# One more weight tile in the ring: nine tiles of 8 KB a partition instead of eight, in a one-core RG-LRU / gated-MLP / mixture-of-experts kernel

## The chip, the cores and the metric

The kernel runs as one program on one core of a Trainium2 chip. The metric is the device time of one execution in microseconds (us); lower is better. Engines are called by the profile's names: PE is TensorE's matmuls and PEld its weight loads, DVE is VectorE, ACT is ScalarE, POOL is GpSimd and SP is SyncE, which here issues nearly all transfers from HBM. A transfer issued by SP carries one weight tile of 1 MB (128 partitions x 2048 floats).

## The reference, cut to what matters

Two layers over 256 latent tokens of width 1024. Layer 0 mixes tokens with a bidirectional recurrent block (RG-LRU), layer 1 with a gated MLP over chunks of 128 tokens; each is followed by a mixture of experts, which is where most of the weights are.

```python
def moe_ffn(xn, router_w, router_b, w_gu, w_down, ws_gu, ws_down):   # xn: 256 x 1024
    scores = jax.nn.sigmoid(xn @ router_w)                           # 64 experts
    ...                                                              # the best 4 of 8 groups, of those the best 8 experts
    y = lax.map(expert_block, ...)       # swiglu(x_pad[tok], w_gu[e], w_down[e]) * gate
    return routed + swiglu(xn, ws_gu, ws_down)                       # and one shared expert
```

An expert has `w_gu` (1024 x 512) and `w_down` (256 x 1024) in float32: three tiles of 1 MB. All 64 experts of both layers are read once, so a mixture of experts reads 192 MB of expert tiles and 3 MB of the shared expert's.

## The kernel before, in words

**The ring.** Every weight goes through one stream, `Stream`. The order of its loads is fixed when the program is written: `moe_loads` and the lists around it call `st.add`. A load takes the slot that was freed longest ago; SP is in order, so a load whose slot is still in use holds every later load. The slots are the `RING` tiles named `wr`, and from the end of layer 0's mixer on four more named `wx`: 12 slots in both mixtures of experts, and 13 after the change. Expert loads cannot be issued before the router has written `order` (the experts in order of load), because their addresses come from it.

**A mixture of experts, `moe(l, tail)`.** Work of three kinds shares PE:

- Experts with few tokens are packed: a group `g` has four blocks of 32 token slots, from one to four experts, which run side by side on PE. `gate_up` does a group in two halves (four of eight 128-row pieces each, one `w_gu` tile per expert and half), `flip` and `down` do the second product, `gather` and `scatter` move the tokens of a batch of two groups in and out by matmuls with one-hot matrices. There are 22 groups in 11 batches, and before a batch the tiles of its experts are taken from the stream in a fixed order.
- Two experts (`NAT`) and the shared one are computed for all tokens, and so are the five experts with most tokens (`TOP`). This work is cut into pieces that can be put anywhere, the queue `ups`: per expert one entry that starts splitting its first weight tile, 16 steps of gate and up product (`over_all`, 6 matmuls a step), again an entry that starts the split, and two steps of the down product (`all_down`, 24 matmuls each).
- These dense experts use weights split in a high and a low part: `splitter` copies a quarter tile to `wh` on ACT (line 563), and POOL or DVE subtract it to give `wl` (line 564). Splitting runs two to three quarter tiles ahead of PE, but the first quarter of an expert's gate and up tiles, and of its down tile, is asked for by the entry that starts it. Below, such a first quarter is called a **restart**.

**What sets the order around the change.** While the program is written, a planner keeps a clock (`st.now`, advanced by the table `COST`) and an expected arrival for each load: 2.6 us after the later of the load before it and the moment its slot was freed. Before a piece of group work, `until` takes steps from `ups` until the tiles of that piece should have arrived:

```python
        def until(tiles):
            while ups:
                t = max(st.arrival(n) for n in tiles)
                if t <= st.now:
                    break
                ...
                up(1)
            st.now = max(st.now, max(st.arrival(n) for n in tiles))
```

So the number of slots changes not only when a load may be issued but where the dense experts' steps stand in every engine's program. Once written, the order is fixed; each engine waits by semaphores.

Of the kernel before, what the change touches and what calls it, by code (L numbers as in the profile page):

```python
# [20 lines left out]
T = 256  # L21
E = 64
EPS = 1e-6
RING = 8

NEXT = (0, 2, 2)

# [274 lines left out]
def _body(nc, tc, a, pp, rp, ps, ps1, dr):  # L302
# [334 lines left out]
    def mixer0(rx):  # L637
      with tc.tile_pool(name="m0", bufs=1) as mp, tc.tile_pool(name="m0t", bufs=2) as tp:
# [24 lines left out]
        nc.sync.dma_start(mixg, a["mix_g"])  # L663
        st.grow(rp, "wr", RING)
        for t_, n_ in ((cw, "a_cw"), (cb, "a_cb"), (rb_, "a_rb"), (ib_, "a_ib"), (lam, "a_lam")):
# [956 lines left out]
```

## Time and profile before

| | |
|---|---|
| time, median of 3 runs | 1508.54 us (1504.59 to 1512.67) |
| the profiled execution, its own time | 1504.02 us |
| span of its profile, first to last instruction | 1502.2 us |
| mean granted TensorE clock | 0.973 of 2.4 GHz |
| PE busy | 1410.3 us (94%) |
| bytes over the transfers' queues | 514.88 MB, mean 343 GB/s |
| layer 0: mixer, then mixture of experts | to about 293 us, to about 803 us |
| layer 1: mixer, then mixture of experts | to about 991 us, to about 1496 us |

The profile shows one execution. A row of a timeline gives start, duration, engine, line, operation, tiles and count; a bracket at its end says how long the engine had been idle and which instruction ended that. The clock column (PEclk) is the share of 2.4 GHz that TensorE was granted: 1.00, or 0.5 (1.2 GHz), or a mean of both over a stretch.

### The profile page before, as it was taken

To read this page: it belongs to the slowest core of one execution; us is meant where nothing else is said; L and a number is where in the kernel's file an instruction comes from. 1 tells how busy PE (TensorE), PEld (TensorE's weight loads), DVE (VectorE), ACT (ScalarE), POOL (GpSimd) and SP (SyncE) were. 2 spreads that over 40 slices of the span, in tenths; PEclk is the share of its full clock that TensorE was granted. 3 is DMA by queue.
4 is the path that set the end of the run, shared out by engine and by line. 5 is a ranking of instruction groups with operands and counts; after the bars stand their busy time and mean duration, and the time that the engine had idled before them with its cause. 6 is when DMAs were issued, how large, how long until landed. Compare 5 with 4: busy or idle time off the path is not lost.

```text
span 1502.2 us, 27457 instructions
## 1 busy us (share of the span) xinstructions
PE 1410.3 (94%) x10752; PEld 983.3 (65%) x10752; DVE 766.5 (51%) x1388; ACT 518.9 (35%) x901; POOL 433.7 (29%) x454
## 2 busy tenths in 40 slices
PE   5999898789999999999999999789999999999998
PEld 4767677546567565565747899666656666566665
DVE  6899997623343434334346686532425333333434
ACT  4767673321222222222225544422212212212232
POOL 1666665412222113221101361322212212211210
PEclk9999999899999999999999999899999999999998
DMA  9776575589998999999999854469998999999994
GB/s 376 280 278 228 224 308 224 231 318 377 381 418 358 421 420 406 421 394 420 420 418 380 320 169 153 140 231 391 362 396 358 421 421 409 406 402 422 420 420 168
DMA packets 77446, 514.88 MB, mean 343 GB/s; under 512 B 9856, under 2 KB 10240, under 8 KB 17024
## 3 DMA queue, kind: packets, MB, share of 16 engines
q1 hardware_dynamic: 74720, 508.91, 83.8%
q10 hardware_dynamic: 2592, 4.16, 0.8%
q8 instruction: 86, 1.41, 0.4%
q14 instruction: 48, 0.39, 0.1%
HBM read 511.99 MB, written 1.05 MB: 342 GB/s over the span
## 4 chain that ended last, share of the span: by engine, by line
PE 59%; issue 13%; POOL 3%; DVE 2%; DMA 2%; ACT 1%; ACTq 0%; POOLq 0%; SPq 0%; DVEq 0%
PE b L307 49%; PE s L307 10%; DMA wr<-in_m_gu 2%; POOL S L1399 1%; POOL wl L564 1%; PE b L1475 1%; DMA wr<-in_m_dn 1%; DVE wl L564 1%; DVE h L948 0%; ACT wh L563 0%; PE b L1587 0%; DVE v L1004 0%; DVE xT L1115 0%; DVE v L1067 0%; DVE u L956 0%
## 5 line engine op out<-in xcount | busy, mean ns | idle before, releaser
L564 POOL TENSOR_TENSOR wl<-wr,wh 128x512 fp32r<-128x512 f32 x134 | 208.2, 1570 | 537.0 <-ACT wh L563 534.8
L307 PE MATMUL b<-wr,xg 128*32 128x512 f32 (+2 forms) x1496 | 301.1, 602 | 8.2 <-DMA wr<-in_m_gu 6.3
L563 ACT CAST wh<-wr 128x512 fp32r<-128x512 f32 x256 | 152.4, 618 | 200.8 <-PE b L307 93.6
L307 PE MATMUL b<-wx,xg 128*32 128x512 f32 (+1 forms) x712 | 196.1, 599 | 0.0
L307 PEld LDWEIGHTS b<-wr,xg 128*32 128x32 f32 (+2 forms) x1496 | 83.3, 119 | 130.6 <-issue 107.2
L307 PE MATMUL s<-hh,wh 128*128 128x256 f32 x512 | 153.7, 300 | 6.4 <-ACT wh L563 6.4
L564 POOL TENSOR_TENSOR wl<-wx,wh 128x512 fp32r<-128x512 f32 x48 | 71.4, 1505 | 302.5 <-ACT wh L563 263.5
L1115 DVE SCALAR_TENSOR_TENSOR xT<-b,mod,xT 128x256 f32<-128x256 f32 x304 | 130.0, 478 | 49.1 <-PE b L307 43.2
L564 DVE TENSOR_TENSOR wl<-wr,wh 128x512 fp32r<-128x512 f32 x122 | 100.2, 838 | 104.3 <-ACT wh L563 104.2
L1491 DVE SCALAR_TENSOR_TENSOR Y<-b,gt,Y 128x512 fp32r<-128x512 f32 x88 | 66.1, 751 | 169.4 <-ACT Y L1490 169.4
L307 PE MATMUL s<-hh,wl 128*128 128x256 f32 x512 | 146.9, 287 | 3.4 <-POOL wl L564 3.4
L307 PE MATMUL b<-wr,ht 128*32 128x512 f32 (+2 forms) x752 | 148.1, 599 | 1.5 <-ACT ht L1477 1.4
L307 PE MATMUL s<-hl,wh 128*128 128x256 f32 x512 | 145.9, 285 | 0.0
L1468 DVE TENSOR_TENSOR h<-h,b 128x256 f32<-128x256 f32 x44 | 18.5, 420 | 205.3 <-ACT h L1467 205.3
L307 PEld LDWEIGHTS s<-hh,wh 128*128 128x128 f32 x512 | 99.4, 194 | 36.0 <-issue 28.3
L1490 ACT ACTIVATE Y<-b,gt 128x512 fp32r<-128x512 f32 x88 | 60.5, 687 | 136.0 <-PE b L307 136.0
L1467 ACT ACTIVATE h<-b 128x256 f32<-128x256 f32 x44 | 16.9, 383 | 256.4 <-PE b L307 256.4
L307 PEld LDWEIGHTS s<-hh,wl 128*128 128x128 f32 x512 | 99.4, 194 | 4.5 <-POOL wl L564 4.2
L307 PEld LDWEIGHTS s<-hl,wh 128*128 128x128 f32 x512 | 99.6, 194 | 0.4
L307 PE MATMUL b<-wx,ht 128*32 128x512 f32 (+2 forms) x352 | 99.1, 603 | 0.5 <-ACT ht L1477 0.5
L563 ACT CAST wh<-wx 128x512 fp32r<-128x512 f32 x112 | 66.5, 618 | 93.9 <-PE b L307 48.3
L1399 POOL TENSOR_SCALAR S<-cst,agq 128x32 fp32r<-128x32 f32 (+3 forms) x208 | 82.6, 421 | 49.4 <-PE b L307 49.3
(283 smaller groups left out, 2817.5 us busy)
## 6 DMA issues: line engine op xcount, KB each, us to landing
wr<-in_m_gu SPq DMA_DIRECT2D x173, 1024.0 KB, 11.6
wx<-in_m_gu SPq DMA_DIRECT2D x83, 1024.0 KB, 11.9
wr<-in_m_dn SPq DMA_DIRECT2D x82, 1024.0 KB, 10.8
wx<-in_m_dn SPq DMA_DIRECT2D x40, 1024.0 KB, 9.9
wr<-in_ada_w SPq DMA_DIRECT2D x31, 1024.0 KB, 7.8
wr<-in_a_in SPq DMA_DIRECT2D x10, 1024.0 KB, 8.7
wr<-in_ada SPq DMA_DIRECT2D x8, 1024.0 KB, 12.2
wr<-in_b_v SPq DMA_DIRECT2D x7, 1024.0 KB, 16.3
```

What stands on the lines that cost most here:

```text
L307: PE.matmul(out, lhsT, rhs, start=start, stop=stop, skip_group_check=True)
L563: S.copy(out=hi, in_=t)
L564: eng(i, c).tensor_tensor(out=lo, in0=t, in1=hi.bitcast(F32), op=OP.subtract)
L1115: V.scalar_tensor_tensor(out=xT[:, d, :], in0=y, scalar=mod[:, l, 5, d:d + 1], in1=xT[:, d, :], op0=OP.mult, op1=OP.add)
L1399: (G if b else V).tensor_scalar(out=s[:, tt, i * P + o:i * P + o + wd], in0=C["iota1"][:, j:j + wd], scalar1=agq[:, tt, q:q + 1], scalar2= ...
L1467: S.activation(out=h, in_=p[:, :256], func=AF.Silu)
L1468: V.tensor_tensor(out=h, in0=h, in1=p[:, 256:], op=OP.mult)
L1475: PE.transpose(p[:, k * P:(k + 1) * P], h[:, k * P:(k + 1) * P], ident)
L1490: S.activation(out=hi, in_=p, func=AF.Copy, scale=gts[g])
L1491: V.scalar_tensor_tensor(out=y[:, 1, 512 * c:512 * c + 512], in0=p, scalar=gts[g], in1=hi.bitcast(F32), op0=OP.mult, op1=OP.subtract)
```

## The change

`RING` becomes 9, and the program is built with 1 KB a partition set aside for the descriptors of transfers that GpSimd issues, instead of the builder's default, which makes room for the 8 KB of the ninth tile. The kernel issues no transfer from GpSimd. No arithmetic changes, and no transfer is added or removed.

```diff
-RING = 8
+RING = 9
...
-    nc = bacc.Bacc("TRN2", target_bir_lowering=False, num_devices=1)
+    nc = bacc.Bacc("TRN2", target_bir_lowering=False, num_devices=1, dynamic_dma_scratch_size=1024)
```

The planner then writes a different order. Three places are shown, all in layer 0's mixture of experts; layer 1's has the same differences.

SP, the start of the expert loads. `wr` and `wx` are ring tiles, `order` is the router's list and `flag` the word that tells whether an expert has more tokens than its slots. Before, the last load ahead of the wait for `flag` (the fourth):

```order
L382 DMA wx_2611<-in_m_gu 128x2048
L374 TENSOR_LOAD order
L374 ISA x2
L382 ISA
L382 DMA wr_2681<-in_m_gu 128x2048
L1357 TENSOR_LOAD flag
```

With nine:

```order
L382 DMA wr_2611<-in_m_gu 128x2048
L374 TENSOR_LOAD order
L374 ISA x2
L382 ISA
L382 DMA wr_2622<-in_m_gu 128x2048
L374 TENSOR_LOAD order
L374 ISA x2
L382 ISA
L382 DMA wx_2692<-in_m_gu 128x2048
L1357 TENSOR_LOAD flag
```

A fifth expert tile is loaded ahead of the flag; every later load has moved one place up against the work that frees slots.

ACT, around the first four-expert group. `hf` and `fh` end the gate and up product of a dense expert, `wh` is the high part of a split quarter tile, `h` and `ht` belong to a group's activation and transpose, `xg` is a gather's result, `Y` a down product's. Before:

```order
L1170 ACTIVATE hf<-s 128x512
L1174 CAST fh<-hf 128x512
L563 CAST wh<-wx_2217 128x512 x4
L1467 ACTIVATE h<-b 128x256
L1477 COPY ht<-b 128x256
L1415 COPY xg<-b 128x512
L1490 ACTIVATE Y<-b,gt 128x512 x2
L1477 COPY ht<-b 128x256
L1415 COPY xg<-b 128x512
L563 CAST wh<-wx_2284 128x512
```

With nine:

```order
L1170 ACTIVATE hf<-s 128x512
L1174 CAST fh<-hf 128x512
L1467 ACTIVATE h<-b 128x256
L1477 COPY ht<-b 128x256
L1415 COPY xg<-b 128x512
L1490 ACTIVATE Y<-b,gt 128x512 x2
L1477 COPY ht<-b 128x256
L1415 COPY xg<-b 128x512
L563 CAST wh<-wr_2139 128x512 x3
L1490 ACTIVATE Y<-b,gt 128x512 x2
```

The restart of the next dense expert (`wx_2217`, and `wr_2139` with nine) has moved from right behind the end of the one before it to behind the second gather.

PE, the third of the five top experts. `s<-hh` and `s<-hl` are its last gate and up step, `b<-fh` and `b<-fl` the first matmuls of its down product, and `b<-wx,xg` a group's gate and up matmuls. Before:

```order
L307 MATMUL s<-hh,wh 128x256
L307 MATMUL s<-hl,wh 128x256
L307 MATMUL s<-hh,wl 128x256
L307 MATMUL b<-fh,wh 128x256
L307 MATMUL b<-fl,wh 128x256
L307 MATMUL b<-fh,wl 128x256
```

With nine:

```order
L307 MATMUL s<-hh,wh 128x256
L307 MATMUL s<-hl,wh 128x256
L307 MATMUL s<-hh,wl 128x256
L307 MATMUL b<-wx_6075,xg 32x512
L307 MATMUL b<-wr_6154,xg 32x512
L307 MATMUL b<-wr_6165,xg 32x512
```

A half group (16 such matmuls) now stands between the end of this expert's first product and the start of its second.

## Rows read from the trace of the kernel before

**Rows 1.** The page: busy time, and the granted clock in 40 slices of the span.

```profile
PE 1410.3 (94%) x10752; PEld 983.3 (65%) x10752; DVE 766.5 (51%) x1388; ACT 518.9 (35%) x901; POOL 433.7 (29%) x454
PEclk9999999899999999999999999899999999999998
```

**Rows 2.** Stretches of layer 0's experts: length, busy time (and count) of five engines, clock, DMA share, GB/s.

```profile
314.50:781.90 467.40, 454.71 (x3632) 292.60 (x3634) 178.91 (x333) 114.93 (x207) 97.12 (x138) 0.99 0.98 403
470.00:535.00 65.00, 64.97 (x479) 39.49 (x471) 23.43 (x44) 15.31 (x28) 12.11 (x23) 1.00 1.01 421
535.00:782.00 247.00, 241.00 (x1973) 156.59 (x1975) 96.31 (x181) 61.07 (x110) 49.34 (x66) 0.99 1.00 414
```

**Rows 3.** Timeline of SP, which only issues: start, duration of the issue, tiles.

```profile
276.28 0.34 SPq L382 DMA_DIRECT2D wx<-in_m_gu  x1
297.19 0.34 SPq L382 DMA_DIRECT2D wr<-in_m_gu  x1
300.63 0.34 SPq L382 DMA_DIRECT2D wr<-in_m_gu  x1
309.72 0.33 SPq L382 DMA_DIRECT2D wx<-in_m_gu  x1
310.31 1.52 SPq L382 DMA_DIRECT2D wr<-in_m_gu  x3
```

**Rows 4.** The chain that ended last: start, duration, and what it was then.

```profile
300.63 4.62 DMA wr<-in_m_gu
311.48 12.00 DMA wr<-in_m_gu
327.46 10.25 DMA wr<-in_m_dn
729.25 7.21 PE s L307 x60
1091.53 3.57 PE b L307 x32
```

**Rows 5.** Timeline of PE, layer 0, first four-expert group.

```profile
305.29 1.06 PE L307 MATMUL b<-wr,xg 128*32 128x512 f32 x1 [2.34 <-DMA wr<-in_m_gu]
316.96 0.38 PE L307 MATMUL s<-hh,wh 128*128 128x256 f32 x1 [2.02 <-ACT wh L563]
318.32 0.38 PE L307 MATMUL s<-hh,wl 128*128 128x256 f32 x1 [0.86 <-POOL wl L564]
```

**Rows 6.** Waits of PE, layer 1, 995 to 1042 us: total, times, longest.

```profile
PE b L307 <- DMA wr<-in_m_gu: 2.4, 1, 2.4
```

**Rows 7.** Timeline of PE, layer 0, later restarts.

```profile
384.65 0.39 PE L307 MATMUL s<-hh,wh 128*128 128x256 f32 x1 [1.19 <-ACT wh L563]
386.00 0.39 PE L307 MATMUL s<-hh,wl 128*128 128x256 f32 x1 [0.85 <-POOL wl L564]
568.03 0.38 PE L307 MATMUL b<-fh,wh 128*128 128x256 f32 x1 [1.19 <-ACT wh L563]
635.82 0.39 PE L307 MATMUL b<-fh,wh 128*128 128x256 f32 x1 [2.74 <-ACT wh L563]
637.18 0.58 PE L307 MATMUL b<-fh,wl 128*128 128x256 f32 x1 [0.75 <-POOL wl L564]
```

**Rows 8.** Stretches around those rows, columns as in rows 2.

```profile
301.20:311.00 9.80, 7.46 (x36) 1.81 (x33) 1.33 (x4) 0.32 (x1) 0.00 (x0) 0.83 0.37 115
383.00:391.00 8.00, 5.96 (x38) 3.72 (x41) 2.42 (x3) 2.76 (x5) 6.33 (x11) 0.79 0.95 377
566.00:574.00 8.00, 5.96 (x47) 5.55 (x47) 4.43 (x8) 2.76 (x5) 5.95 (x9) 1.00 1.02 424
632.00:644.00 12.00, 8.51 (x50) 6.58 (x52) 5.86 (x9) 4.01 (x7) 4.20 (x3) 0.72 1.01 413
```

**Rows 9.** Waits of PE, layer 0, 535 to 790 us: total, times, longest.

```profile
PE b L307 <- ACT wh L563: 3.9, 2, 2.7
PE b L307 <- POOL wl L564: 1.6, 2, 0.9
```

## The prediction, made before the changed kernel had run

> **What bounds the kernel now.** I read the page first: PE is busy 94% of the span, and its granted clock is nearly always full [rows 1]. PE is therefore the engine to watch, and a change to loads can only pay where PE waits for a load. The kernel's mixers are left out for that reason; the ring is stretched to its limit in the two mixtures of experts, where the queue runs at 0.98 of its time at 403 GB/s (the first row of [rows 2]).
>
> Next, stretches of layer 0's experts. From 470 to 535 us both sides are full: PE 64.97 of 65 us, the queue 421 GB/s. From 535 to 782 the queue still moves 414 GB/s and PE is busy 241 of 247 us [rows 2]. Two things full at once do not tell which one waits for the other, so the waits decide. In 535 to 790 us PE waited for splits of dense experts (ACT `wh`, POOL `wl`: 3.9 and 1.6 us) and never for a load worth a row [rows 9]. At the start of the experts it did wait for loads: 2.34 us before 305.29 in layer 0 [rows 5], 2.4 us in layer 1 [rows 6], and the chain runs over transfers there three times [rows 4]. So loads bound the first 40 us or so of each mixture, PE's own order of work the rest.
>
> One full-rate tile takes 1.0486 MB / 421 GB/s = 2.49 us. A lone tile lands 4.62 us after its issue [rows 4]. A half of a four-expert group costs PE 3.57 us, and one dense step 7.21 / 10 = 0.72 us [rows 4].
>
> **The change, part by part.** *(a) The fifth expert tile ahead of the flag.* Before, SP issues three expert tiles up to 276.28, a fourth soon after, and the next at 297.19, when the first group has freed a slot; the one that PE then waits for goes at 300.63 [rows 3]. With nine, the tile of 297.19 is already in, and the awaited one takes its place: 297.19 + 4.62 = 301.8, before 302.95 (305.29 - 2.34), where PE ran dry. The gap of 2.34 us goes [rows 5], and with it the half-rate clock behind it: 9.8 us at 0.83 cost 1.7 us [rows 8]. The half that ended in the release of 309.72 [rows 3] now ends 4.0 us earlier, at 305.7.
>
> That release sends the second half's tiles. Before, four were issued, the last landing at 311.48 + 12.00 = 323.48 [rows 4]; now one of them went early, and the third of a release lands 323.48 - 2.49 - 309.72 = 11.3 us behind it, at 317.0. The half starts 6.5 us earlier. But the planner has taken three dense steps (2.2 us) out of the fill in front of it, because it books 2.6 us a tile and not the 4.62 of a queue that had run dry. Six steps (4.3 us) end near 310, so **PE idles some 6 us for loads where it idled 2.02 + 0.86 us for a restart** [rows 5]. After that the half clock (1.2 GHz) is likely: 0 to 1.7 us.
>
> The down tiles follow the next release as before (327.46 + 10.25, [rows 4]) and keep the lead; the restart that moved behind the second gather is covered by that wait. One more step is put off. Gain of layer 0: 6.5 less four deferred steps (2.9) less 0 to 1.7 = 1.9 to 3.6, I take 2.7. Layer 1 has the gap [rows 6] but I found no slow clock behind it: 2.4 + 2.5 - 2.9 less 0 to 1.7 = 0.3 to 2.0, taken as 1.1. Together **3.8 us (2.2 to 5.6)**.
>
> *(b) The restarts.* PE's work does not change, so from there on only its idle time and clock count. In layer 0 before, after the first group: one restart behind a gather at 384 (1.19 + 0.85 us, and 8 us at 0.79 of the clock, 1.7 us), one behind a gather at 568 (1.19 and a POOL part of 1.6 - 0.75 = 0.85 us, clock full), and the third top expert's, directly behind the end of its own first product (2.74 + 0.75, and 12 us at 0.72, 3.4 us) [rows 7 to 9]. Sum 3.7 + 2.0 + 6.9 = 12.6 us. None of these three stands there with nine: the first follows a down product, the second a half group comes between, the third likewise.
>
> The new order exposes five. Two down products begin right behind the end of another expert's first product, as the restart of [rows 5] did: 2.88 us each. Two top experts begin behind a gather: 2.04 us each. The one behind a down product is not in the trace: at least 1 us (a copy on ACT has to wait for that product's `Y`), at most 2.04; I take 1.5, since ACT has less queued than behind a gather. Sum 11.3 us. The clock: after the four long gaps of layer 0 before it fell to a cost of 1.7, 0 and 3.4 [rows 8] and some in the first; I take 1.7 in two of the five (14.7 us), none to all five (11.3 to 19.8). Against 12.6 that is 2.1 us lost a layer (1.3 won to 7.2 lost), **4.2 us lost in both (2.6 won to 14.4 lost)**.
>
> *(c) The rest, at nothing.* The small transfers that now stand behind a ninth tile at the program's start land one tile later, 2.49 us if nothing covered it; I take nothing, since their first use comes later than that. The smaller area for GpSimd's descriptors costs nothing, since the kernel gives GpSimd no transfer. Earlier loads of the late experts are worth nothing while PE does not wait for them; if PE got far ahead, the full queue would be next (403 of 421 GB/s).
>
> **Sum:** 3.8 - 4.2 = 0.4 us slower, between 8.2 us faster and 12.2 us slower. The sum is made on the profiled execution, 1504.02 us; the median of the runs shown is 1508.54, 0.3% above it, and I put the same difference on it: **1509 us**. This measurement cannot tell less than 0.5% (7.5 us) from no change.
>
> **The rivals.** *Restarts fall well:* the clock stays full and the exposed restarts coincide with waits for loads. Both upper bounds then hold, 8.2 us, 1500 us. For it: the clock did stay full at 568 [rows 8]. Against it: PE is late there, not the loads. Chance 0.2.
>
> *The queue's idle time comes back:* between 314.5 and 781.9 us the queue moves 403 and not 421 GB/s, so it loses 467.4 x (1 - 403/421) = 20 us a layer; if loads bound the layer, a deeper ring gives both back: 1509 - 40 = 1469 us. Against it stands the list of waits without a load [rows 9]. The Trainium skill (Perfetto Trace Analysis, Optimization Strategy) says that consistent bubbles on the engine that should be saturated can mean that there is not enough SBUF for the next tile. By that rule the change should win; here the bubbles of PE after 535 us end with a split, not with a load, so the trace agrees only for the start. Chance 0.1.
>
> *Slower:* the new wait of (a) recurs. The planner moves steps away from in front of tiles wherever it now expects them sooner, and a tile is sooner only if its slot was the limit and the queue not full. Where it was full, four deferred steps (2.9 us) turn into a wait, with 1.7 us of clock. With two such places more in each layer: 2 x 2 x 4.6 = 18 us, 1527 us. It decides from two places a layer upward. For it: 470 to 535 us, where queue and PE are both full [rows 2]. Against it: the tiles in front of which steps were taken away were bought one release earlier. Chance 0.16.
>
> *The change doesn't act:* the orders shown differ in every engine, so 0.02, same time.
>
> **How the numbers follow.** The likeliest case, no measurable change at 1509, has 0.52. Its own range is 1500 to 1521, the two ends of the sum. Faster by over 0.5% (under 1501) are the queue's case and most of the well-falling restarts: 0.1 + 0.18 = 0.28. Slower (over 1516) is 0.16; the likeliest case's tail to 1521 is small beside it. Within 0.5%: 0.56. The range 1494 to 1523 leaves out the queue's case and about half of the slow one, less than 0.2.
>
> **What would show each step.** For (a): the fifth expert tile issued before 285 us; PE's gap at 305 gone; a new gap of 5 to 7 us before the second half of the first four-expert group, ended by a load. For (b): the gap of 2.74 us at 636 gone, and gaps of 2 to 3 us at restarts elsewhere, five a layer, with the half clock behind some. I would be wrong if PE waits for loads in the middle of the experts, if the restarts are hidden or cost more than a split and a subtraction, or if PE's busy time itself falls or grows by more than the clock explains.

## The result: slower by 0.6%, and the profile after

The changed kernel takes 1516.52 us (median of 8 runs, 1515.49 to 1518.06) against 1507.26 us before (8 runs); the ratio is 1.0062, with a 95% interval of 1.0046 to 1.0078. The forecast was 1509 us in a range of 1494 to 1523. The range holds the result. The likeliest case, no change beyond 0.5%, does not: the loss is some 9 us where the sum said 0.4. It is clear of the noise: with eight runs of each kernel the interval is 0.16% to either side, finer than the 0.5% that the prediction allowed for.

The page of the changed kernel, to set beside [rows 1]; its span is 1514.8 us, against 1502.2:

```profile
PE 1410.4 (93%) x10752; PEld 979.3 (65%) x10752; DVE 769.0 (51%) x1388; ACT 518.3 (34%) x901; POOL 434.2 (29%) x454
PEclk9999999899999999999999999899999999999998
```

PE's busy time and its count are those of before, so the 12.6 us of span look like idle time. Over layer 0's experts as a whole the queue moves less than before (395 against 403 GB/s); only from 535 us on it moves a little more (418 against 414). Stretches, for [rows 2]:

```profile
314.50:787.00 472.50, 454.02 (x3609) 290.02 (x3608) 176.90 (x328) 113.70 (x205) 96.90 (x138) 0.98 0.96 395
...
535.00:787.00 252.00, 247.37 (x1996) 159.35 (x1995) 97.91 (x183) 61.14 (x111) 49.34 (x66) 0.99 1.01 418
```

**The start.** SP in the timeline, for [rows 3]; the last number is the count of issues in the row:

```profile
274.97 3.29 SPq L382 DMA_DIRECT2D wr<-in_m_gu  x4
281.96 0.34 SPq L382 DMA_DIRECT2D wx<-in_m_gu  x1
```

The fifth expert tile goes at 281.96 instead of 297.19. PE's waits in the timeline, for [rows 5] (layer 0, first two rows) and [rows 6] (layer 1):

```profile
313.98 1.04 PE L307 MATMUL b<-wr,xg 128*32 128x512 f32 x2 [2.48 <-DMA wr<-in_m_gu]
316.47 1.06 PE L307 MATMUL b<-wx,xg 128*32 128x512 f32 x1 [1.45 <-DMA wx<-in_m_gu]
...
1017.51 1.05 PE L307 MATMUL b<-wr,xg 128*32 128x512 f32 x2 [1.77 <-DMA wr<-in_m_gu]
1019.99 1.06 PE L307 MATMUL b<-wx,xg 128*32 128x512 f32 x1 [1.44 <-DMA wx<-in_m_gu]
```

The gap at 305 us is gone. The next half group waits for its tiles instead, as step (a) said. The wait is longer than its gaps: the half's own stretch, from its first matmul to its last, shows 10.60 us with 6.68 us busy; the same 32 matmuls (the program's 16, each of which the trace lists as two) take 4.60 us where nothing is waited for, at much the same clock (the first experiment below). That is 6.0 us of waiting, of which the trace books 3.9 as idle:

```profile
310.50:321.10 10.60, 6.68 (x48) 1.67 (x48) 1.38 (x2) 0.62 (x1) 0.00 (x0) 0.84 0.84 352
```

**The restarts.** PE in the timeline, for [rows 7], layer 0: the restart behind the second gather, then the five behind it.

```profile
330.65 0.39 PE L307 MATMUL s<-hh,wh 128*128 128x256 f32 x1 [1.19 <-ACT wh L563]
332.01 0.38 PE L307 MATMUL s<-hh,wl 128*128 128x256 f32 x1 [0.85 <-POOL wl L564]
...
368.92 0.39 PE L307 MATMUL b<-fh,wh 128*128 128x256 f32 x1 [2.74 <-ACT wh L563]
370.26 0.51 PE L307 MATMUL b<-fh,wl 128*128 128x256 f32 x1 [0.84 <-POOL wl L564]
394.42 0.38 PE L307 MATMUL s<-hh,wh 128*128 128x256 f32 x1 [1.37 <-ACT wh L563]
453.05 0.58 PE L307 MATMUL b<-fh,wh 128*128 128x256 f32 x1 [2.74 <-ACT wh L563]
613.45 0.39 PE L307 MATMUL s<-hh,wh 128*128 128x256 f32 x1 [1.19 <-ACT wh L563]
666.75 0.39 PE L307 MATMUL s<-hh,wh 128*128 128x256 f32 x1 [1.19 <-ACT wh L563]
```

All five stand where the order put them; layer 1 has the same five. Stretches of 10 us around them, for [rows 8]: three with the clock below 1.00 in layer 0, four in layer 1.

```profile
366.00:376.00 10.00, 6.42 (x42) 5.00 (x44) 5.75 (x9) 2.90 (x6) 2.95 (x2) 0.83 0.68 269
450.00:460.00 10.00, 6.70 (x34) 6.20 (x33) 5.99 (x11) 3.42 (x6) 2.97 (x3) 0.66 0.75 296
612.00:622.00 10.00, 7.96 (x51) 3.44 (x50) 2.59 (x4) 3.84 (x7) 6.76 (x12) 0.83 1.01 417
665.00:675.00 10.00, 7.96 (x69) 6.52 (x71) 3.24 (x4) 4.01 (x7) 6.41 (x8) 1.00 1.01 419
...
1366.00:1376.00 10.00, 7.96 (x53) 7.55 (x51) 2.67 (x4) 4.00 (x7) 5.20 (x5) 0.83 1.01 420
```

The list of PE's waits from 340 to 790 us, for [rows 9] (total, times, longest):

```profile
PE b L307 <- ACT wh L563: 5.5, 2, 2.7
PE s L307 <- ACT wh L563: 3.8, 3, 1.4
PE s L307 <- POOL wl L564: 2.5, 3, 0.9
PE b L307 <- POOL wl L564: 1.4, 2, 0.8
PE b L307 <- DVE wl L564: 0.8, 1, 0.8
...
PE b L307 <- DMA wr<-in_m_gu: 0.4, 1, 0.4
```

These are 14.0 us for splits and 0.4 for loads. One of them, 0.8 us for DVE, is no new one: the kernel before has it too. In layer 1 (1040 to 1493 us) the splits sum to 14.3 us.

### The profile page after: what moved, and what is told of

The parts are those of the page before. It is cut to its first block, busy times and chain, and to the rows that moved or that the text cites. A ratio compares the mean times of both kernels' runs of the same rounds, so it can differ in the third digit from the quotient of the medians.

```text
span 1514.8 us, 27436 instructions
## 1 busy us (share of the span) xinstructions
PE 1410.4 (93%) x10752; PEld 979.3 (65%) x10752; DVE 769.0 (51%) x1388; ACT 518.3 (34%) x901; POOL 434.2 (29%) x454
## 4 chain that ended last, share of the span: by engine, by line
PE 56%; issue 18%; POOL 3%; DVE 2%; DMA 1%; ACT 1%; ACTq 0%; POOLq 0%; DVEq 0%
PE b L307 44%; PE s L307 11%; POOL wl L564 1%; POOL S L1399 1%; DMA wr<-in_m_gu 1%; PE b L1475 1%; DVE wl L564 1%; DVE h L948 0%; DVE xT L1115 0%; DVE v L1004 0%; PE b L1587 0%; DVE v L1067 0%; DVE u L956 0%; ACT wh L563 0%; ACT h L1066 0%
## 5 line engine op out<-in xcount | busy, mean ns | idle before, releaser
L564 POOL TENSOR_TENSOR wl<-wr,wh 128x512 fp32r<-128x512 f32 x136 | 215.3, 1601 | 611.2 <-ACT wh L563 580.7
L307 PE MATMUL b<-wr,xg 128*32 128x512 f32 (+2 forms) x1440 | 307.0, 605 | 5.9 <-DMA wr<-in_m_gu 4.7
L307 PE MATMUL b<-wx,xg 128*32 128x512 f32 (+2 forms) x768 | 220.6, 603 | 3.6 <-DMA wx<-in_m_gu 2.9
L563 ACT CAST wh<-wr 128x512 fp32r<-128x512 f32 x272 | 161.5, 618 | 180.7 <-PE b L307 109.9
L564 DVE TENSOR_TENSOR wl<-wr,wh 128x512 fp32r<-128x512 f32 x136 | 117.0, 877 | 101.7 <-ACT wh L563 101.6
L564 POOL TENSOR_TENSOR wl<-wx,wh 128x512 fp32r<-128x512 f32 x46 | 65.1, 1430 | 262.0 <-ACT wh L563 222.5
L307 PE MATMUL b<-wx,ht 128*32 128x512 f32 (+2 forms) x392 | 117.8, 600 | 0.5 <-ACT ht L1477 0.5
L307 PEld LDWEIGHTS b<-wx,xg 128*32 128x32 f32 (+2 forms) x768 | 55.4, 117 | 70.8 <-issue 59.0
L307 PE MATMUL b<-S,xt 128*128 128x256 f32 x704 | 94.0, 287 | 0.0
## 6 DMA issues: line engine op xcount, KB each, us to landing
wr<-in_m_gu SPq DMA_DIRECT2D x170, 1024.0 KB, 11.8
wx<-in_m_gu SPq DMA_DIRECT2D x86, 1024.0 KB, 11.3
wr<-in_ada SPq DMA_DIRECT2D x8, 1024.0 KB, 14.4
```

Source lines behind the costliest of these rows:

```text
L307: PE.matmul(out, lhsT, rhs, start=start, stop=stop, skip_group_check=True)
L563: S.copy(out=hi, in_=t)
L564: eng(i, c).tensor_tensor(out=lo, in0=t, in1=hi.bitcast(F32), op=OP.subtract)
```

## The experiments

The change does two things, a ninth slot and a new order of steps. The theory to test (A): the slot gains at the start, and the order loses at the restarts. Its rivals: the slot or the smaller descriptor area hurts by itself (B), or loads bound the experts, so that a gain at one place is lost at the next load (C).

### The slot, the order and the descriptor area apart

Nine tiles with the order of eight: the number of entries of `ups` (dense steps, and the entries that start a split) that `until` takes at each of its 66 calls in a layer is written out as a table, taken from the kernel before.

```diff
+        steps = iter([
+            0, 0, 0, 10, 0, 2, 2, 2, 7, 3, 0, 4, 2, 2, 0, 5, 0, 2, 2, 2, 4, 7,
...
+        ])
         def until(tiles):
-            while ups:
...
+            up(next(steps))
             st.now = max(st.now, max(st.arrival(n) for n in tiles))
```

> Nine tiles in the ring, but the dense experts' steps stand where they stood with eight (the number of steps before each piece of group work is written out as a table). Theory A (the loss comes from where the reorder leaves the restarts): the splits cost what they cost before (11 to 12 us of idle PE a layer, clock at half some 8 us a layer), and the load gaps at the start of each mixture of experts (2.34 us and 2.42 plus 1.04 us) go or shrink below 1 us: 1500 to 1505 us, 3 to 7 us faster than with eight. Rival B (the ninth tile itself hurts, by its place in memory or by the transfers it adds in flight): near the changed kernel, 1514 to 1518 us. Rival C (the start gives nothing either): 1507 us as before.

Measured: 1490.36 us, ratio 0.988 (0.986 to 0.9899). The direction is A's, and B is out. The gain, 16.6 us, is far above the 3 to 7 expected, and 1490 lies outside A's range. The two halves of the second group, by stretches of this kernel:

```profile
301.10:305.80 4.70, 4.70 (x34) 1.17 (x34) 1.48 (x4) 0.56 (x2) 0.00 (x0) 1.00 0.71 253
317.20:321.80 4.60, 4.60 (x49) 1.38 (x51) 0.05 (x1) 0.00 (x0) 0.00 (x0) 0.80 0.97 367
```

Before, the first of these took some 9.5 us ([rows 8], first row), 4.8 more. The expectation counted the idle gap of 2.34 us of it; the half clock behind the gap makes some 1.7, and the last 0.8 is a wait inside PE's busy time. Over the whole execution such hidden waits are the larger part: the span is 13.2 us shorter (1489.0 against 1502.2), and of these PE's busy time gives 8.7 (1401.6 against 1410.3, [rows 1]), with the same 10752 matmuls and nearly the same mean clock (0.974 and 0.973).

Eight tiles with the order of nine (the same edit in the kernel before, with the other table):

> Eight tiles in the ring, with the dense experts' steps where they stand with nine: the reorder alone. Theory A: the same split gaps as in the changed kernel (about 16 us a layer against 11), and since a load that the new order counts on is one release later, longer load gaps at the start of each mixture of experts, 6 to 10 us a layer against 3.5: 1520 to 1536 us, slower than the changed kernel. Rival B (the ninth tile hurts by itself, the order does not): 1507 us, as before. If the reorder costs its splits and no more load time: 1516 us.

Measured: 1541.24 us, ratio 1.0226 (1.0208 to 1.0245). The waits of PE in layer 0, 300 to 804 us:

```profile
PE b L307 <- DMA wr<-in_m_gu: 7.2, 6, 2.5
PE b L307 <- ACT wh L563: 5.5, 2, 2.7
PE s L307 <- ACT wh L563: 4.9, 4, 1.4
PE s L307 <- POOL wl L564: 3.4, 4, 0.9
...
```

The split waits are those of the changed kernel (this list begins at 300 us and so has the first restart too), and load waits come on top, as A expects; the sum is 5 us above its range, again with a busy time that has grown (1429.3 us). The four corners:

| | order of eight | order of nine |
|---|---|---|
| eight tiles | 1507 us | 1541.2 us |
| nine tiles | 1490.4 us | 1516.5 us |

The ninth tile gains 17 us in one order and 25 in the other. The new order loses 34 and 26.

The descriptor area alone, cut to 1 KB with eight tiles:

> The kernel before with eight tiles and only the descriptor area cut to 1 KB. Theory A: no change, ratio 0.998 to 1.002, 1507 us, and the same gaps of PE in both mixtures of experts. Rival B (the smaller area or the moved addresses of the tiles cost time): 1510 us or more, with longer transfers or longer copies on ACT, DVE and POOL.

Measured: 1506.17 us, ratio 0.9991 (0.998 to 1.0003). No cost is to be seen.

### Where in the order the 26 us lie

Nine tiles, with the new order only at the start of each mixture of experts: the table of eight with 6 instead of 10 entries before the second group's second half, and 11 instead of 7 before the fourth group's first. (The 10 are nine dense steps and the entry that starts the next expert's split.)

```diff
-            0, 0, 0, 10, 0, 2, 2, 2, 7, 3, 0, 4, 2, 2, 0, 5, 0, 2, 2, 2, 4, 7,
+            0, 0, 0, 6, 0, 2, 2, 2, 11, 3, 0, 4, 2, 2, 0, 5, 0, 2, 2, 2, 4, 7,
```

> Nine tiles, splits as before, the new order only up to the fourth group of each mixture of experts and the order of eight from there on: the four steps that the new order takes away from in front of the second group's second half are done before the fourth group's first half. Theory A (the reorder loses little at the start and most at the five restarts after it): from 1490.4 us, load gaps of 3.9 and 3.2 us come back, the first restart costs 0.8 us less in each layer, half clock 0 to 3.4 us: 1495 to 1500 us, leaving 16 to 21 us of the reorder's 26 for the restarts after it. Rival C (the start carries most of it): 1505 us or more.

Measured: 1502.15 us, ratio 0.9968 (0.9956 to 0.9981). Of the 26.2 us the start carries 11.8 and the order behind it 14.4. That is in neither expected range, about midway between them: A is right that the order behind the start carries the larger part, and wrong that the start loses little. The list of PE's waits from 340 to 790 us for splits, to be read against the one of the changed kernel above:

```profile
PE b L307 <- ACT wh L563: 3.9, 2, 2.7
PE b L307 <- POOL wl L564: 2.2, 3, 0.8
PE s L307 <- ACT wh L563: 1.2, 1, 1.2
...
PE s L307 <- POOL wl L564: 0.8, 1, 0.8
PE b L307 <- DVE wl L564: 0.8, 1, 0.8
```

8.9 us here, 14.0 in the changed kernel: 5.1 us of idle time more; in layer 1 the same sums are 8.9 and 14.3.

The half clock differs too. In this run it stands behind two restarts in each layer, 1.7 us each time; the two of layer 0:

```profile
564.00:574.00 10.00, 7.96 (x52) 7.50 (x50) 4.66 (x9) 2.76 (x5) 7.62 (x14) 0.83 1.01 421
634.00:644.00 10.00, 8.41 (x56) 5.49 (x56) 4.38 (x7) 3.06 (x6) 4.24 (x3) 0.83 1.00 411
```

The first of these is the restart that in the trace of before kept the full clock ([rows 8], third row), in the same order of work and with the same waits. The reverse is seen in the run with the smaller area alone, where the restart at 384 us waits as before (1.19 and 0.84 us) and keeps the full clock, against 0.79 in [rows 8]:

```profile
383.00:391.00 8.00, 6.00 (x50) 3.17 (x50) 2.75 (x3) 3.45 (x6) 6.82 (x12) 1.00 0.95 373
```

So which restart is followed by the half clock is no property of the order; it changes from one execution to another.

### The restarts made earlier

The changed kernel with PE's order kept to the row. Only the first two splits of a restart move: ahead of the last two steps of the first product in front of it, or right behind the second step of the down product in front of it.

```diff
+        def early(i):
+            fn, n, cost, at = ups[i]
+            if n is not None and cost == 0.0 and st.arrival(n) <= st.now:
+                ups[i] = (lambda: None, n, 0.0, None)
+                fn()
+
         def up(n):
             for _ in range(n):
                 if ups:
+                    if len(ups) > 2 and ups[0][2] and ups[0][3] is None and ups[1][3] is None:
+                        early(2)
                     fn, tile_, cost, at = ups.popleft()
...
                     fn()
                     st.now += cost
+                    if at and ups:
+                        early(0)
```

> The changed kernel with PE's order kept, but each dense expert's first two quarter tiles are split earlier: before the last two steps of the first product ahead of it, or right behind the second step of the down product ahead of it, if the tile is expected to be there. Theory A (late splits are what the change lost): the gaps of 1.19 and 0.85 us behind gathers and of 1.37 and 0.85 us behind a down product go, those of 2.74 us shrink to 2.3 to 2.5 us, since the chain that ends the first product is nearly as long, and lose the 0.85 us behind them; 8 to 10 us of idle PE a layer and 3 to 7 us of half clock a layer: 1484 to 1498 us, below the kernel with eight. Rival C (loads bound the experts, so that what is won at a split is lost at the next load): new load gaps in the middle of the experts, 1507 us or more.

Measured: 1469.77 us, ratio 0.9747 (0.973 to 0.9764): 46.7 us below the changed kernel and 14 below A's range. PE's waits in layer 0, 300 to 767 us:

```profile
PE b L307 <- DMA wr<-in_m_gu: 2.5, 1, 2.5
PE b L307 <- DMA wx<-in_m_gu: 1.4, 1, 1.4
PE b L307 <- POOL wl L564: 0.8, 1, 0.8
PE b L307 <- DVE wl L564: 0.8, 1, 0.8
...
```

The stretch behind the start of layer 0's experts, in the changed kernel (340 to 790 us) and in this one (336.2 to 766.6, the same 3491 matmuls):

```profile
340.00:790.00 450.00, 435.02 (x3491) 279.61 (x3493) 171.62 (x321) 106.58 (x192) 90.12 (x126) 0.98 0.98 401
```

```profile
336.20:766.60 430.40, 428.26 (x3491) 279.01 (x3494) 167.06 (x321) 108.00 (x192) 88.72 (x126) 1.00 1.00 413
```

Idle time falls from 15.0 to 2.1 us, and the clock is full throughout, which takes 6.8 us off the busy time, just what the three half-clock stretches above had cost (1.7 + 3.4 + 1.7). The 2.74 us gaps go whole, against the expectation that 2.3 to 2.5 us of each would stay. ACT in the changed kernel shows why; the restart of 368.92:

```profile
365.51 0.60 ACT L1170 ACTIVATE hf<-s 128x512 f32<-128x512 f32 x1 [8.64 <-PE s L307]
367.73 0.62 ACT L1174 CAST fh<-hf 128x512 fp32r<-128x512 f32 x1 [1.62 <-DVE hf L1173]
368.25 1.66 ACT L563 CAST wh<-wr 128x512 fp32r<-128x512 f32 x3
```

The split was not waiting for its tile. It stood on ACT behind `fh`, which ends another expert's product and waits 1.62 us for DVE; the down product that restarts is that of the expert before, whose `fh` is long there. Where a down product follows its own expert's first product, the gap does stay: in nine tiles with the order of eight (below) one row has 2.22 us behind `fh` itself.

The same edit in the kernel before:

> The kernel before, eight tiles and its own order on PE, with the earlier splits of the dense experts. Theory A (restarts cost their idle time and the half clock behind it, wherever they stand): idle PE for splits falls from 11 us a layer to 2 or 3, and of the half clock behind the six long restarts (13.6 us in both layers) most goes: 1475 to 1483 us. With the run of nine tiles and earlier splits (1469.8) that leaves nine tiles with the new order 5 to 13 us ahead of eight, where it was 9 us behind. Rival C (with eight tiles the time won at splits is lost again at loads): 1490 us or more, with new load gaps.

Measured: 1492.25 us, ratio 0.9906 (0.9886 to 0.9927). A's range is missed, C's bound of 1490 is met. The waits in layer 0, 300 to 775 us:

```profile
PE b L307 <- DMA wr<-in_m_gu: 5.3, 4, 2.3
...
PE b L307 <- DMA wr<-in_m_dn: 1.4, 1, 1.4
...
```

With eight tiles PE, no longer held up at splits, runs into loads: 6.7 us against 3.1 before in this layer (300 to 783 us). So C holds for eight tiles, in part.

Nine tiles, the order of eight, and the earlier splits:

> Nine tiles, the order of eight, and the earlier splits. Theory A: from 1490.4 us, 20 us of idle PE for splits and 7 to 10 us of half clock go: 1458 to 1466 us. Against nine tiles with their own order and earlier splits (1469.8) it is faster by the load gaps at the start of each mixture of experts alone, 3.9 and 3.2 us, and up to 3.4 us of half clock. Rival B (the new order is better once its splits are hidden): 1470 us or more.

Measured: 1464.55 us, ratio 0.9727 (0.9706 to 0.9748), as A expected. The order that cost 26.2 us costs 5.2 once the splits are early. The row with `fh`:

```profile
616.81 0.38 PE L307 MATMUL b<-fh,wh 128*128 128x256 f32 x1 [2.22 <-ACT fh L1182]
```

### The planner's booking of an empty queue

The changed kernel's planner takes steps away in front of the second half of the second group because it books 2.6 us for a tile whose slot comes free when nothing is in flight. A lone tile takes 4.62 us [rows 4]. One line books 2.2 us more in that case; `open` is the time at which `order` is ready.

```diff
-            self.dma = max(self.dma, self.since.get(w, 0.0)) + LOAD
+            self.dma = max(self.dma, max(self.since.get(w, 0.0), self.open) + 2.2) + LOAD
```

With this alone:

> The changed kernel with one thing added: the planner books 2.2 us more for a load whose slot comes free when the queue has run dry; splits stay as they were. It writes ten dense steps in front of the second group's second half as the order of eight does. Theory A (the reorder was the loss, and this booking undoes it): near the run of nine tiles with the order of eight (1490.4), 1484 to 1497 us. Rival (any order planned for nine tiles leaves its restarts as badly): 1505 us or more.

Measured: 1485.81 us, ratio 0.9855 (0.9829 to 0.988), 31 us below the changed kernel and in A's range. Ten entries (nine steps) stand in front of the second group's second half again, in both layers. The line changes the order behind the start as well, so the 31 us are those of the whole order, not of this one place. With the earlier splits as well:

> Nine tiles, earlier splits, and a planner that books 2.2 us more for a load whose slot comes free when the queue has run dry (a lone tile lands 4.6 to 4.9 us after its issue in the traces). It writes ten dense steps instead of six in front of the second group's second half, and a similar order to that of eight tiles from there on. Theory A: the load gaps at the start go, the splits stay hidden: 1458 to 1466 us. Rival (they come back in front of another tile): 1469 us or more, as with nine tiles, their own order and earlier splits.

Measured: 1460.23 us, ratio 0.9692 (0.9672 to 0.9712), in A's range. PE's waits in layer 0, 300 to 761 us, and the whole of that stretch:

```profile
PE b L307 <- DMA wx<-in_m_gu: 1.4, 1, 1.4
PE s L307 <- DVE wl L564: 0.9, 1, 0.9
...
300.00:761.00 461.00, 456.40 (x3718) 291.37 (x3720) 176.56 (x337) 117.23 (x209) 93.84 (x138) 1.00 1.00 412
```

Both mends with eight tiles, and with ten. With 1 KB a partition for descriptors ten tiles do not fit, by 0.97 KB a partition; with the area cut to 32 bytes they do.

> Eight tiles with both mends, the earlier splits and the booking of an empty queue. Theory A (with splits hidden, loads at the start of each mixture of experts are what is left, and the ninth tile is worth what it was with the order held, 17 to 28 us): 1477 to 1488 us against 1460.2 with nine. Rival (the mends alone do it, the ninth tile is worth nothing once order and splits are right): 1458 to 1465 us.

> Ten tiles with both mends, the area for descriptors cut to 32 bytes a partition to make room. With nine (1460.2), PE waits for loads only 1.44 us in each mixture of experts, so a tenth can give 3 us and what clock follows: 1452 to 1460 us. Rival (the reorder by a tenth tile exposes something again): 1465 us or more.

Measured: 1475.29 us, ratio 0.9793 (0.9772 to 0.9815), with eight, a little below A's range; and 1453.64 us, ratio 0.9655 (0.9638 to 0.9672), with ten, in the expected range. With order and splits mended each further tile pays: 15.1 us for the ninth, some 6 for the tenth, each with the order that the planner writes for it. Ten tiles with both mends is the fastest version, 51 us below the kernel before on the same chip.

## Why the prediction was right in its steps and low in its sum

**What bounds the kernel: right.** Loads bound the start of each mixture, PE's own order the rest. The changed kernel waits 14.0 us for splits after 340 us and 0.4 for loads (layer 0).

**(a) The start: right in its steps; in size only as a sum, and by luck.** The fifth tile, the gap that goes and the wait of "some 6 us" that comes are all in the trace (6.0 us). Term (a) was a gain of 3.8 us, 2.2 to 5.6. The run with the new order at the start and the old one behind it measures 4.7 us (1506.83 - 1502.15). One sentence in it was wrong: the restart behind the second gather is not covered by the wait for down tiles; PE waits 1.19 and 0.85 us for its splits and for no load. The gross gain of the slot, 16.6 us, was larger than the 11.4 us that the working had (6.5 in layer 0, 2.4 + 2.5 in layer 1), and so was the cost of the steps put off, 11.8 us against 5.8 and 0 to 3.4 of clock. The two errors cancel. By layers they do not: from the first group to the place where the steps put off are made up, the same matmuls take 63.2 us before and 62.7 with the new start in layer 0, and 61.9 and 59.9 in layer 1. That is 0.4 and 2.0 us won where the term had 2.7 and 1.1.

**(b) The restarts: right in place, too small in size. This is the term that was mis-sized.** The term was a loss of 4.2 us in both layers; 1516.52 - 1502.15 = 14.4 us was measured, the far end of its range. It has two parts.

- Idle time: five restarts at 11.3 us in place of three at 7.6 us make 3.7 us a layer, 7.5 in both. The waits of the two runs differ by 5.1 and 5.4, together 10.5. The two down products behind another first product wait 2.74 us for the first split and 0.56 to 0.85 for the second, not 2.88 in sum, and the restart behind a down product 1.37 + 0.85, not 1.5 and more than the 2.04 that was named as its most.
- Clock: the term took the half clock behind two restarts a layer, 3.4 us, where before it was 5.1: a gain of 3.4 us in both. The stretches show 1.7 + 3.4 + 1.7 = 6.8 us in layer 0 (10 us at 0.83, 0.66 and 0.83) and four of 1.7 in layer 1: 13.6. The trace of before has 10.2 and that of the run with the new start 6.8, so the loss is 3.4 to 6.8 us, by the execution that it is set against.

So some 3 us of the miss are idle time and 6.8 to 10.2 are clock; with the 4.2 of the term that is 14.0 to 17.4, where the medians differ by 14.4 and the two profiled executions by 15.6 (1516.53 - 1500.97). That the late splits cause both is shown by the run with PE's order unchanged and the splits earlier: both go together there, 15.0 to 2.1 us idle and a clock of 0.98 to 1.00. How many restarts are followed by the half clock could not have been read off one trace: it changes between executions of the same order, as the rows above show.

**(c): right.** The smaller area shows no cost, 0.9991. PE reaches the first group of layer 0 at 293.82 us instead of 293.46, so in these two executions the small transfers at the program's start cost 0.4 us at most.

**The rivals.** *Restarts fall well* is out: none of the five coincided with a load. The time lies just inside what the rival *Slower* claimed (over 1516 us), but not by its mechanism: its new waits for loads do not recur with nine tiles, and the loss is at the restarts. With eight tiles and the same order there are six waits for `wr` tiles in layer 0, 7.2 us, but only 0.9 us of them behind 360 us, so there too they stay at the start. *The queue's idle time comes back* did not happen in the changed kernel (395 GB/s against 403), because the splits held PE first. Once the splits are early and the booking is mended, the queue does carry more, 412 GB/s, and that rival's 1469 us is passed: its mechanism was there behind another bound, but the ring alone did not reach it. The Trainium skill's rule on consistent bubbles (Perfetto Trace Analysis, Optimization Strategy) points the same way: more room for tiles does pay, 16.6 us with the order held. The bubbles that this trace shows behind the start, though, were no lack of room: earlier splits, with the same ring, take 46.7 us off the changed kernel.

## What to carry to other kernels

A buffer that a planner counts changes the program, not only its waits: before judging a deeper ring, run it once with the old order and run the new order once with the old ring, and the two effects (here 17 us won, 26 lost) stand apart. Work that PE starts on only after another engine has prepared it should be prepared ahead of that engine's other work, since an order that hides it by luck is lost at the next edit. A planner's booking must know what a transfer costs in an empty queue; here one line for that was worth 31 us, through the order that it made the planner write.

## What the runs showed of the hardware

- PE's busy time holds waits. The changed kernel and eight tiles in its order run the same 10752 matmuls in the same order at the same mean clock (0.970); PE is busy 1410.4 us in the one and 1429.3 in the other, whose tiles come later. The half group that waits for tiles shows it: 10.60 us long, 6.68 of them busy, where 4.60 are needed. The four experts of a group run side by side, and one whose tile is late leaves PE busy with the others. Busy times at different clocks do not show such waits: both mends have 1384.5 us and the slot alone 1401.6, but at 0.985 and 0.974, and 0.011 of a span of 1489 us is already 16 us.
- The half clock does not follow the length of a gap. In the changed kernel the restarts at 613 and 667 us have the same waits, 1.19 and 0.84 us; the clock in the 10 us around them is 0.83 and 1.00. Nor does it follow the order: the restart at 384 us has 0.79 in one execution and 1.00 in another of the same order.
- The time of a program without transfers from GpSimd did not change when their descriptor area was cut from the builder's default to 1 KB a partition (0.9991, 0.998 to 1.0003); with 32 bytes it still ran.
